# Values centred per head before a delta-rule recurrence, in place of means taken out of its outputs

## The chip, the core and the metric

The kernel runs on one core of a Trainium2 chip. The metric is device time in microseconds (us). The core has five engines that run side by side, each through its own list of instructions in order: TensorE (PE, matrix products), VectorE (DVE), ScalarE (ACT), GpSimd (POOL) and SyncE (SP, which issues most DMAs). An instruction waits on semaphores until what it needs is there, and everything behind it on the same engine waits too.

## What is computed

One layer of a hybrid backbone: 256 context and 1024 latent tokens, width 1024. A projection feeds two branches: (A) a bidirectional recurrence of the RWKV-7 kind with 16 heads of 64 channels, and (B) a bidirectional retention with 4 heads. Both are normed per head, projected, merged by gates and projected once more. What matters here, cut from the reference:

```python
def step(S, inp):                       # branch A, per head; S is (64 values) x (64 keys)
    w_t, k_t, v_t, kk_t, b_t = inp[:5]
    sa = jnp.einsum('bhvk,bhk->bhv', S, kk_t)
    S = (S * w_t[:, :, None, :] - sa[..., None] * b_t[:, :, None, :]
         + v_t[..., None] * k_t[:, :, None, :])
    o = jnp.einsum('bhvk,bhk->bhv', S, inp[5]) if with_out else None
...
o = head_norm((outs[0] + outs[1]).reshape(B, L, A_WIDTH), ln_w, ln_b, A_HEADS, A_GN_EPS)
o = o + (bons[0] + bons[1]).reshape(B, L, A_WIDTH).astype(o.dtype)
```

`head_norm` takes the mean over a head's 64 channels off, divides by the root of their variance, and scales and shifts per channel. The state `S` begins at zero, and each step is linear in `v` along the value axis: decay, the product with the keys and the read-out act on the key axis alone. So if each `v_t` has mean zero over its head's 64 channels, every row sum of `S` and every output `o` has mean zero too. The term `bons` uses `v` itself.

## The kernel before

Tokens lie along the free axis and channels on the 128 partitions, two heads (a "pair") to a tile, so that there are 8 pairs. Products in float32 are made of rounded parts: a tile is split into `hi` (a cast on ACT, line 210) and `lo` (the rest, a subtraction on DVE or POOL, line 211).

**Preparation** (lines 335 to 551, up to about 797 us): for each pair p, `stage_a` projects and convolves keys `kc` and values `vc`, norms the keys, and prepares the values for the recurrence (lines 440 to 457). For each of two directions the values (copied in reversed order for the second one) are transposed on PE in blocks of 128 tokens (line 451), copied from psum into a tile `vt` by ACT (line 452), and stored to the scratch tensor `vtD` by four DMAs on POOL's queue (line 456). `vt` has tokens on its partitions, and 10 blocks of 128 channels, 20 heads' worth of 64, along its free axis. Then come the scaled keys of each direction (`stage_a_dir`), with decays `cs` and products `bk`, `kr` on DVE. Between these, PE runs projections that nothing waits for soon: rope projections of retention's queries and keys (`rope_proj`), and gates. `vt` is one of 11 slots of a pool that most of the tiles of the preparation share.

**Recurrence** (`phase1b`, up to about 1775 us): chunks of 64 tokens, reads `vtD`, sums both directions into `oT` and stores `oD`. PE's order is pinned there.

**Second half** (`phase2`): `retention` goes over 4 heads, in each over chunks of 128 tokens. A chunk's scores are `sc` (line 1469), its output `ro` (lines 1477 and 1416 to 1418), its state update `st` with the result `s` (line 1431) on DVE. The output is normed (lines 1491 to 1496), transposed (`ot`, line 1502), scaled by ACT (`on`, line 1506), gated on POOL and stored to `orD` by SP. `out_a` projects branch A's output. In each of two halves of 512 tokens it first norms 8 tiles, `rwkv_norm` (lines 1296 to 1321): it loads `x`, takes sums over heads with `head_sums`, two products with a block matrix of ones, first of `x` for the mean (`mu`), then of the squares for the variance (`va`). Then it scales, adds the term `bon`, multiplies by the gate, and splits into an `act` tile. All 8 are needed for the projection `ya` (lines 1276 to 1278, 8 outputs of 24 products each per half). Only when retention's buffers are free does `phase3` load its operands: `act` tiles of `orD` (line 1266 ff.) through two buffers `ar`, `fn`, the gate row, `ma`, `mb` and `x`, all on SP's queue. They feed the products `yr`, then the last projection `po`.

What sets the order: the program is written as above, and the framework's scheduler interleaves it into one list per engine before the run, by its own model of durations. In the second half, retention, the norms and `ya` are therefore mixed on each engine.

The shared helper and the norm's own lines:

```python
def head_sums(self, acc, x, hl, eng=None):
    hi, lo = hl
    self.split(hi, lo, x, eng)
    self.nc.tensor.matmul(acc, self.ones, hi, start=True, stop=False)
    self.nc.tensor.matmul(acc, self.ones, lo, start=False, stop=True)
```

Of the kernel before, what the change touches and what calls it, by code (L numbers as in the profile page):

```python
# [8 lines left out]
F32 = mybir.dt.float32  # L9
F32R = mybir.dt.float32r  # L10
AF = mybir.ActivationFunctionType
ALU = mybir.AluOpType
# [3 lines left out]
P = 128  # L16
# [4 lines left out]
T = CTX + LAT  # L21
NPAIR = 8
C = 64
NU = T // C
# [19 lines left out]
MUE = 1  # L44
# [84 lines left out]
class Kern:  # L129
# [282 lines left out]
    def stage_a(self, p, wp, gps, bonus):  # L412
        nc, pv = self.nc, self.pv
        col = lambda base: pv[:, base + p:base + p + 1]
        ur = self.sa.tile([P, 2, 2, P], F32, tag="st", name=self.nm("ur"), bufs=3)
        nc.sync.dma_start(ur, self.ins["lup"][p])
        uh = self.l1.tile([P, 2, 2, P], F32R, tag="uph", name=self.nm("uph"), bufs=1)
        ul = self.upl
        nc.scalar.copy(uh, ur)
        nc.vector.tensor_tensor(ul[0:64], ur[0:64], uh[0:64].bitcast(F32), op=ALU.subtract)  # L420
        self.up = uh, ul
        kc = self.conv_proj(8 + p, 8 + p, False, wp, gps, "kc")
        self.filler_tile()
        vc = self.conv_proj(16 + p, 16 + p, False, wp, gps, "vc")
        self.filler_tile()
        bonus()

        sq = self.slot("sq")
        nc.scalar.activation(sq[:, :T], kc[:, :T], AF.Square, scale=col(PV_KK))
        hi, lo, rn = self.slot("sh", F32R), self.slot("sl", F32R), self.slot("rn")  # L430
        for (t0, n) in BLOCKS:
            a = self.aps.tile([P, 512], F32, tag="a", name=self.nm("ssk"))
            b = slice(t0, t0 + n)
            self.head_sums(a[:, :n], sq[:, b], (hi[:, b], lo[:, b]), SSE and nc.gpsimd)
            nc.scalar.activation(rn[:, t0:t0 + n], a[:, :n], AF.Ln, bias=self.eps[:, 3:4])
        nc.scalar.activation(rn[:, :T], rn[:, :T], AF.Exp, scale=-0.5)
        kk = self.slot("kk")
        nc.vector.scalar_tensor_tensor(kk[:, :T], kc[:, :T], col(PV_KK), rn[:, :T], op0=ALU.mult, op1=ALU.mult)

        for d in range(2):  # L440
            src = vc
            if d == 1:
                src = self.slot("vr")
                for a, b in ((0, CTX), (CTX, T)):
                    nc.scalar.copy(src[:, a:b], vc[:, a:b][:, ::-1])
            vt = self.slot("vt")
            for q in range(0, 10, 4):
                m = min(4, 10 - q)
                tp = self.tps.tile([P, 512], F32, tag="t", name=self.nm("vtp"))
                for i in range(m):  # L450
                    nc.tensor.transpose(tp[:, i * P:(i + 1) * P], src[:, (q + i) * P:(q + i + 1) * P], self.ident)
                nc.scalar.copy(vt[:, q * P:(q + m) * P], tp[:, :m * P])
            v4 = vt[:, :T].rearrange("q (t h c) -> q t h c", h=2, c=C)
            for h in range(2):
                for par in range(2):
                    nc.gpsimd.dma_start(self.vtD[p, d, h].rearrange("q (t a) c -> q t a c", a=2)[:, :, par, :],
                                        v4[64 * par:64 * par + 64, :, h, :])
        rc = self.conv_proj(p, p, True, wp, gps, "rc")
        self.filler_tile()
        kds = None  # L460
        for d in range(2):
            kds = self.stage_a_dir(p, d, kc, kk, rc, kds)
            self.filler_tile()
        self.gate_proj(24 + p, self.gD[p], True, wp, gps, self.sa)
        self.filler_tile()

        nc.vector.scalar_tensor_tensor(kds[:, CTX:T], kds[:, CTX:T], col(PV_RK), rc[:, :LAT], op0=ALU.mult, op1=ALU.mult)

        def bonus():
            bon, hi, lo = self.slot("bon"), self.slot("bh", F32R), self.slot("bl", F32R)  # L470
            for b in range(2):
                a = self.aps.tile([P, 512], F32, tag="a", name=self.nm("bon"))
                c = slice(512 * b, 512 * b + 512)
                self.head_sums(a, kds[:, CTX:][:, c], (hi[:, c], lo[:, c]), BNE and nc.gpsimd)
                nc.vector.scalar_tensor_tensor(bon[:, 512 * b:512 * b + 512], a, 0.5, vc[:, CTX + 512 * b:CTX + 512 * b + 512],
                                               op0=ALU.mult, op1=ALU.mult)
            nc.gpsimd.dma_start(self.bonD[p], bon[:, :LAT])
        return bonus
# [817 lines left out]
    def rwkv_norm(self, p, t0, ps):  # L1296

        nc = self.nc
        col = lambda base: self.ph[:, base + p:base + p + 1]
        psum = lambda name: ps.tile([P, 512], F32, tag="ps", name=self.nm(name), bufs=2)  # L1300
        x = self.ap.tile([P, 512], F32, tag="ar", name=self.nm("ar"), bufs=AR)
        self.load(x, self.oD[p][:, t0:t0 + 512])
        parts = lambda: [self.wp.tile([P, 512], F32R, tag=t, name=self.nm(t), bufs=b) for t, b in (("hi", WH), ("lo", WH))]
        pm = psum("mu")
        self.head_sums(pm, x, parts(), MUE and nc.gpsimd)
        nc.vector.scalar_tensor_tensor(x, pm, -1.0 / 64, x, op0=ALU.mult, op1=ALU.add)
        sq = self.wp.tile([P, 512], F32, tag="sq", name=self.nm("sq"), bufs=1)
        nc.scalar.activation(sq, x, AF.Square)
        pq = psum("va")
        self.head_sums(pq, sq, parts(), VAE and nc.gpsimd)  # L1310
        nc.scalar.activation(sq, pq, AF.Ln, bias=self.eps[:, 1:2], scale=1.0 / 64)
        nc.scalar.activation(sq, sq, AF.Exp, scale=-0.5)
        nc.vector.tensor_tensor(x, x, sq, op=ALU.mult)
        nc.vector.tensor_scalar(x, x, col(PV_LW), col(PV_LB), op0=ALU.mult, op1=ALU.add)
        for src, op in ((self.bonD, ALU.add), (self.gD, ALU.mult)):
            t = self.wp.tile([P, 512], F32, tag="ma", name=self.nm("bg"), bufs=2)
            self.load(t, src[p][:, t0:t0 + 512])
            nc.gpsimd.tensor_tensor(x, x, t, op=op)
        hl = self.ap.tile([P, 2, 512], F32R, tag=f"a{p}", name=self.nm("act"), bufs=1)
        self.split(hl[:, 0], hl[:, 1], x)  # L1320
        return hl
# [276 lines left out]
```

## Time and profile before

| | us |
|---|---|
| median of three runs | 2483.74 (2483.72 to 2492.42) |
| the profiled execution: its time | 2488.66 |
| its span, first to last instruction | 2486.9 |
| mean granted TensorE clock | 0.988 |
| PE busy, 100 to 300 us | 199.2 of 200 |
| DVE busy, 100 to 300, 300 to 500, 500 to 700 | 144.3, 154.1, 152.2 of 200 each |
| DVE busy, 1800 to 1900 | 84.5 of 100 |

The profile is of one execution. Its page gives busy time per engine; other views group instructions by line, operation and tile, list who waited for whom, show instructions in order of time, or give busy time by stretches. Names are the program's tile names: `mu<-hi,ones` is a product that writes `mu` from `hi` and `ones`. PEld is PE's loading of weights, which overlaps its products. A line can be that of a helper, so tiles tell more than lines. Queue issues appear as SPq or POOLq.

### The profile page before, as it was taken

The numbers are of one execution on the slowest core, as the hardware profiler recorded it, in microseconds if no ns is written. First come the engines' busy times: TensorE is split into PE (matmuls) and PEld (weight loads), VectorE is DVE, ScalarE is ACT, GpSimd is POOL, SyncE is SP. The second block draws the span as 40 slices with busy tenths as digits, with TensorE's granted clock in tenths as the row PEclk, the third lists the DMA queues.
The fourth block names the chain that finished last, engine by engine and source line by source line (L and its number), as shares of the span: only waits on it lengthen the run. The fifth ranks groups of instructions, "written<-read, shape, count | busy, mean of one in ns | idle before, by whom it ended". The sixth has DMA issues, their size and how long they took to land. (4 is left out here: it accounts for less than half of the span.)

```text
span 2486.9 us, 53478 instructions
## 1 busy us (share of the span) xinstructions
PE 2387.7 (96%) x21200; PEld 1926.9 (77%) x21200; DVE 1596.5 (64%) x2834; ACT 1159.9 (47%) x2547; POOL 575.0 (23%) x720
## 2 busy tenths in 40 slices
PE   7999999999999999998999999999898998999998
PEld 4888888888888899887777777777665765678786
DVE  5486787777666334353988777883378558745644
ACT  6434344434443444445665566644355435533422
POOL 2221111112122011111232222222276345400000
PEclk9999999999999999998999999999999999999999
DMA  6154454445446525344655566553465654575552
GB/s 251 50 161 116 138 163 132 131 151 142 127 143 191 175 73 147 99 135 131 171 161 173 151 180 180 157 159 116 132 200 175 204 170 152 169 272 178 182 174 85
DMA packets 337709, 385.07 MB, mean 155 GB/s; under 512 B 87467, under 2 KB 240819, under 8 KB 334387
## 3 DMA queue, kind: packets, MB, share of 16 engines
q1 hardware_dynamic: 304370, 298.80, 39.3%
q0 software_dynamic: 12992, 55.58, 8.5%
q10 hardware_dynamic: 20096, 27.27, 3.1%
q8 instruction: 167, 2.74, 0.5%
q14 instruction: 84, 0.68, 0.1%
HBM read 264.63 MB, written 116.92 MB: 153 GB/s over the span
## 5 line engine op out<-in xcount | busy, mean ns | idle before, releaser
L330 PE MATMUL gm<-uh,wh 128*128 128x512 f32 x896 | 351.2, 393 | 5.6 <-ACT xp L402 3.6
L331 PE MATMUL gm<-ul,wh 128*128 128x512 f32 x896 | 351.6, 392 | 0.7 <-DVE ul L299 0.7
L332 PE MATMUL gm<-uh,wl 128*128 128x512 f32 x896 | 351.2, 392 | 0.0
L1065 POOL TENSOR_TENSOR sp<-sv,pc 64x256 f32<-64x256 f32 x152 | 104.8, 690 | 428.4 <-DVE sv L1089 192.2
L330 PEld LDWEIGHTS gm<-uh,wh 128*128 128x128 f32 x896 | 168.1, 188 | 40.0 <-ACT xp L402 4.0
L331 PEld LDWEIGHTS gm<-ul,wh 128*128 128x128 f32 x896 | 168.4, 188 | 37.9 <-DVE xnt L298 1.7
L332 PEld LDWEIGHTS gm<-uh,wl 128*128 128x128 f32 x896 | 168.3, 188 | 34.3
L557 PE MATMUL gm<-uh,wlo 128*128 128x512 f32 x416 | 171.1, 411 | 0.7 <-DVE wlo L660 0.7
L557 PE MATMUL gm<-uh,whi 128*128 128x512 f32 x416 | 171.1, 411 | 0.0
L557 PE MATMUL gm<-ul,whi 128*128 128x512 f32 x416 | 170.7, 410 | 0.0
L660 DVE TENSOR_TENSOR wlo<-wraw,whi 128x256 fp32r<-128x256 f32 x168 | 79.2, 483 | 126.0 <-ACT whi L659 125.5
L557 PE MATMUL gv<-wlo,uh 128*128 128x256 f32 x512 | 148.4, 290 | 0.6 <-issue 0.6
L557 PE MATMUL gv<-whi,ul 128*128 128x256 f32 x512 | 148.5, 290 | 0.3 <-issue 0.3
L557 PE MATMUL gv<-whi,uh 128*128 128x256 f32 x512 | 148.1, 289 | 0.0
L211 DVE TENSOR_TENSOR lo<-raw,hi 128x512 fp32r<-128x512 f32 x128 | 92.6, 732 | 84.1 <-ACT hi L210 83.8
L210 ACT CAST hi<-raw 128x512 fp32r<-128x512 f32 x128 | 78.0, 620 | 130.1 <-PE yr L1277 62.3
L904 DVE TENSOR_TENSOR TL<-TL,tmp 128x31 f32<-128x31 f32 (+15 forms) x310 | 129.8, 419 | 8.1
L902 DVE TENSOR_TENSOR tmp<-E,TL 128x31 f32<-128x31 f32 (+15 forms) x310 | 129.2, 417 | 8.8
L1079 ACT COPY uv<-U 64x256 f32<-64x256 f32 x160 | 58.7, 367 | 149.6 <-PE U L557 87.0
L1477 PE MATMUL ro<-s,rs 128*128 128x512 f32 x256 | 123.4, 597 | 1.8 <-DVE s L1431 1.8
L1089 DVE TENSOR_TENSOR sv<-S,sp 64x256 f32<-64x256 f32 x144 | 60.7, 422 | 94.8 <-PE S L557 71.4
L210 ACT CAST wh<-wr 128x1024 fp32r<-128x1024 f32 x56 | 58.8, 1050 | 130.6 <-PE gm L331 103.3
(297 smaller groups left out, 6208.0 us busy)
## 6 DMA issues: line engine op xcount, KB each, us to landing
wr<-in_w_in SPq DMA_DIRECT2D x56, 512.0 KB
wraw<-in_w_in SPq DMA_DIRECT2D x84, 256.0 KB
bk<-bkD SPq DMA_DIRECT2D x80, 256.0 KB
krD<-kr POOLq DMA_DIRECT2D x16, 1024.0 KB, 4.6
raw<-in_wr SPq DMA_DIRECT2D x64, 256.0 KB
vtD<-vt POOLq DMA_DIRECT2D x64, 160.0 KB, 4.2
bkD<-bk POOLq DMA_DIRECT2D x32, 320.0 KB, 6.6
bkD<-bk POOLq DMA_DIRECT2D x16, 640.0 KB, 6.4
```

The costliest lines, as they stand in the source:

```text
L210: nc.scalar.copy(hi, src)
L211: (eng or nc.vector).tensor_tensor(lo, src, hi.bitcast(F32), op=ALU.subtract)
L330: nc.tensor.matmul(acc[:, :n], hi[:, k, :], self.hi(k, t0, n), start=(k == 0), stop=False)
L331: nc.tensor.matmul(acc[:, :n], hi[:, k, :], self.lo(k, t0, n), start=False, stop=False)
L332: nc.tensor.matmul(acc[:, :n], lo[:, k, :], self.hi(k, t0, n), start=False, stop=(k == KT - 1))
L557: return self.pin(self.nc.tensor.matmul(*a, **k))
L660: self.late(nc.vector.tensor_tensor(lo[:, j % size, k:k + 2], r, h.bitcast(F32), op=ALU.subtract), "v")
L902: self.late(nc.vector.tensor_tensor(t3, et[:, j + 1:, j:j + 1].broadcast_to([P, n, m]), tl[:, j:j + 1, 0:m].broadcast_to([P, n, m]), op=AL ...
L904: self.late(nc.vector.tensor_tensor(tl[:, j + 1:, 0:m], tl[:, j + 1:, 0:m], t3, op=ALU.subtract), "v")
L1065: nc.gpsimd.tensor_tensor(sp[ch], sv[ch, h], pcs[ch].broadcast_to([64, 4, C]), op=ALU.mult)
L1089: self.lead("v", nc.vector.tensor_tensor(new[h], ps[ch], sp[ch], op=ALU.add))
L1477: nc.tensor.matmul(po, qx[d][:, k, cols], st[:, k, :], start=(d == 1 and k == 0), stop=False)
```

## The change

In the preparation, after a direction's `vt` is complete, DVE now sums each head's 64 channels of every token (`vm`, 128x20) and subtracts a 64th of the sum in place. The four DMAs to `vtD` now follow that subtraction. In the group norm the mean's two products, their split (a cast on ACT, a subtraction on POOL), their psum tile and the subtraction of the mean on DVE are gone; the squares are taken of `x` as it is loaded. The term with `bon` reads `vc`, which is unchanged. Lines after the first piece are 6 higher in the changed kernel, after the second one 3 higher.

```diff
@@ -450,6 +450,12 @@
                     nc.tensor.transpose(tp[:, i * P:(i + 1) * P], src[:, (q + i) * P:(q + i + 1) * P], self.ident)
                 nc.scalar.copy(vt[:, q * P:(q + m) * P], tp[:, :m * P])
+
+            vm = self.sa.tile([P, NU], F32, tag="vm", name=self.nm("vm"), bufs=2)
+            v3 = vt[:, :T].rearrange("q (u c) -> q u c", c=C)
+            nc.vector.tensor_reduce(vm, v3, axis=mybir.AxisListType.X, op=ALU.add)
+            nc.vector.scalar_tensor_tensor(v3, vm.rearrange("q (u o) -> q u o", o=1).broadcast_to([P, NU, C]), -1.0 / C, v3,
+                                           op0=ALU.mult, op1=ALU.add)
             v4 = vt[:, :T].rearrange("q (t h c) -> q t h c", h=2, c=C)
             for h in range(2):
                 for par in range(2):
@@ -1301,9 +1307,6 @@
         self.load(x, self.oD[p][:, t0:t0 + 512])
         parts = lambda: [self.wp.tile([P, 512], F32R, tag=t, name=self.nm(t), bufs=b) for t, b in (("hi", WH), ("lo", WH))]
-        pm = psum("mu")
-        self.head_sums(pm, x, parts(), MUE and nc.gpsimd)
-        nc.vector.scalar_tensor_tensor(x, pm, -1.0 / 64, x, op0=ALU.mult, op1=ALU.add)
         sq = self.wp.tile([P, 512], F32, tag="sq", name=self.nm("sq"), bufs=1)
         nc.scalar.activation(sq, x, AF.Square)
         pq = psum("va")
```

The scheduler orders each engine's list anew. In the recurrence PE's list stays as it was; in the preparation it moves slightly, and in the second half retention, the norms and `ya` are interleaved in another way. The pieces that matter are shown in the prediction.

## The prediction

> **What bounds the kernel now.** I read the page's first line, then busy time by stretches, then what TensorE (PE) waits for.
>
> ```profile
> PE 2387.7 (96%) x21200; PEld 1926.9 (77%) x21200; DVE 1596.5 (64%) x2834; ACT 1159.9 (47%) x2547; POOL 575.0 (23%) x720
> ```
>
> PE is busy 96% of the span. The timeline shows how long a product really holds it:
>
> ```profile
> 1850.71 0.40 PE L217 MATMUL mu<-hi,ones 128*128 128x512 f32 x1
> 1850.94 1.02 PE L1477 MATMUL ro<-s,rs 128*128 128x512 f32 x2
> ```
>
> The first column is the start, the second the duration. The product lasts 0.40 us, but the next starts 0.23 us later: products overlap, so each costs 0.23 us of the engine's time.
>
> The change adds work in the preparation and takes work out of the second half. The next rows are stretches with us of busy time: length, PE, PEld, DVE (VectorE), ACT (ScalarE), POOL (GpSimd), then the granted clock, DMA share and GB/s.
>
> ```profile
> 300.00:500.00 200.00, 200.00 (x986) 168.14 (x986) 154.09 (x174) 87.65 (x132) 38.92 (x79) 1.00 0.49 139
> 1775.00:1800.00 25.00, 13.20 (x55) 9.98 (x54) 7.92 (x13) 10.68 (x18) 7.24 (x8) 0.80 0.62 184
> 1800.00:1820.00 20.00, 17.26 (x72) 11.35 (x71) 15.97 (x25) 9.44 (x19) 16.51 (x14) 1.00 0.63 198
> 1860.00:1880.00 20.00, 17.11 (x72) 11.45 (x71) 17.24 (x25) 14.31 (x32) 12.88 (x10) 1.00 0.78 231
> 1880.00:1900.00 20.00, 16.30 (x66) 11.19 (x65) 18.59 (x30) 11.11 (x22) 10.78 (x9) 0.92 0.27 86
> 2060.00:2080.00 20.00, 18.26 (x77) 11.98 (x76) 14.85 (x27) 12.70 (x29) 14.23 (x11) 1.00 0.68 213
> 2080.00:2100.00 20.00, 16.79 (x67) 11.98 (x66) 16.96 (x27) 9.54 (x19) 5.74 (x5) 0.91 0.30 95
> 2100.00:2120.00 20.00, 17.95 (x75) 11.58 (x74) 16.84 (x26) 11.77 (x27) 14.65 (x12) 1.00 0.38 115
> ```
>
> In the preparation (first row) PE does not pause at all and DVE has 46 us in 200 free. From 1800 to 2120 PE does pause: in the six rows from 1800 on it is idle 2.7 + 2.9 + 3.7 + 1.7 + 3.2 + 2.1 = 16.3 us. There only retention feeds PE while DVE is up to 93% busy, partly with the group norms.
>
> **What the change removes.** Of each of 16 group norms (8 pairs, 2 halves) go two products, ACT's cast, POOL's subtraction and DVE's removal of the mean.
>
> ```profile
> L210 ACT CAST hi<-ar x16: 607/618/638, 1805.5 to 2126.5; 128x512 fp32r<-128x512 f32 x16
> L1306 DVE SCALAR_TENSOR_TENSOR ar<-mu,ar x16: 665/680/692, 1810.5 to 2133.4; 128x512 f32<-128x512 f32 x16
> ```
> ```profile
> L211 POOL TENSOR_TENSOR lo<-ar,hi 128x512 fp32r<-128x512 f32 x16 | 21.5, 1346 | 28.9 <-ACT hi L210 27.8 <-DMA rs<-kD 1.1
> ```
>
> *PE's work:* 32 x 0.23 = **-7.4 us**, all on the path. *The pauses beside the norms:* 9.9 us of ACT, 10.9 of DVE and 21.5 of POOL go, and each norm's chain is shorter by 0.62 + 1.35 + 0.23 + 0.68 = 2.9 us and its hand-overs. Bounds: none of the 16.3 us, or all. I take **-6 us**, a little over a third, since the rest is retention's own chain. The clock falls to 0.92 and 0.91 in two of these rows: (0.08 + 0.09) x 20 = 3.4 us of cycles, of which I take **-1.5 us**.
>
> **What it adds.** For each of 16 pairs and directions DVE sums 128x1280 into 128x20 and subtracts the mean, between ACT's copies and POOL's stores of `vt`.
>
> ```profile
> L523 DVE SCALAR_TENSOR_TENSOR av<-av,kk 128x1280 f32<-128x1280 f32 x16 | 23.9, 1494 | 0.0
> L521 DVE TENSOR_SCALAR kd<-av,ph 128x1280 f32<-128x1280 f32 x16 | 14.2, 890 | 0.0
> L513 DVE TENSOR_TENSOR_SCAN cs<-scanm,cs 128x650 f32<-128x650 f32 x32 | 46.6, 1498 | 1.4
> ```
>
> The subtraction has L523's form: 1.49 us. A sum of this size is not in the trace: L521 (0.89 us) is its lower end, twice L513's 650 elements (3.0 us) the upper; I take 1.5, nearest to the other pass over 1280 elements. So 16 x 3.0 = 48 us of DVE (38 to 72). The Trainium skill ("VectorE: DVE Perf Modes", section on the perf-mode tier table) says a `tensor_reduce` has only the 1x mode, which at 0.96 GHz is an estimated 1.33 us; with it the 48 would be some 45.
>
> It lies beside PE's work if DVE's gaps hold it. One pair lasts 86 us, from one `kk` to the next (297.27 to 383.76); in brackets is how long DVE had waited:
>
> ```profile
> 297.27 1.55 DVE L438 SCALAR_TENSOR_TENSOR kk<-kc,pv,rn 128x1280 f32<-128x1280 f32 x1 [1.36 <-ACT rn L436]
> 333.79 0.83 DVE L511 TENSOR_SCALAR cs<-cs 128x1280 f32<-128x1280 f32 x1 [1.70 <-ACT cs L507]
> 339.76 1.23 DVE L542 TENSOR_TENSOR kr<-pe,kk 128x1024 f32<-128x1024 f32 x1 [2.12 <-issue]
> 383.76 1.55 DVE L438 SCALAR_TENSOR_TENSOR kk<-kc,pv,rn 128x1280 f32<-128x1280 f32 x1 [6.39 <-ACT rn L436]
> ```
>
> On DVE, pair 2's second direction stood so before (`bk` the scaled keys, `cs` the next direction's decays):
>
> ```order
> L523 SCALAR_TENSOR_TENSOR av_2478<-av_2478,kk_2364 128x1280
> L540 TENSOR_TENSOR kx_2522<-pe_2506,kk_2364 128x256
> L532 TENSOR_TENSOR bk_2515<-kd_2511,pi_2508 128x20x64
> L532 TENSOR_TENSOR bk_2515<-av_2478,pi_2508 128x20x64
> L511 TENSOR_SCALAR cs_2626<-cs_2626 128x20x64
> ```
>
> and now (lines are 6 higher there):
>
> ```order
> L529 SCALAR_TENSOR_TENSOR av_2496<-av_2496,kk_2376 128x1280
> L546 TENSOR_TENSOR kx_2540<-pe_2524,kk_2376 128x256
> L456 TENSOR_REDUCE vm_2422<-vt_2405 128x20
> L538 TENSOR_TENSOR bk_2533<-kd_2529,pi_2526 128x20x64
> L211 TENSOR_TENSOR wl_2867<-wr_2864,wh_2866 128x1024
> L538 TENSOR_TENSOR bk_2533<-av_2496,pi_2526 128x20x64
> L708 SCALAR_TENSOR_TENSOR gp_2759<-gp_2759,gm_2734 128x512
> L457 SCALAR_TENSOR_TENSOR vt_2405<-vm_2422,vt_2405 128x1280
> L517 TENSOR_SCALAR cs_2644<-cs_2644 128x20x64
> ```
>
> The two new rows fall where DVE waited 1.7 and 2.1 us; the first direction's fall into wide gaps between rope tiles. `bk` and `cs` queue behind them, and POOL's four `vtD` stores leave later with `vt`'s slot. Three waits for such a slot exist already:
>
> ```profile
> ACT av L510 <- DMA vtD<-vt: 8.9, 3, 4.1
> ```
>
> (us in all, times, longest). PE has other projections in hand (four psum tiles of 24 products each), so I take **+1.5 us**; bounds 0 and 8 x 2 = 16, a 3.0 us shift of each pair less a third found in gaps.
>
> **What it moves.** PE's order is unchanged through the recurrence. In the second half the norms end sooner, so `ya` starts sooner and is used up sooner. Before, around retention's last product (`ro`; `ot` its transposes, `yr` the next stage):
>
> ```order
> L1416 MATMUL ro_24262<-vt_23692,sx_24259 128x512
> L1417 MATMUL ro_24262<-vt_23692,sx_24259 128x512
> L1418 MATMUL ro_24262<-vt_23692,sx_24259 128x512
> L1502 MATMUL ot_24293<-ident,on_24222 128x128 x4
> L1278 MATMUL ya_25280<-act_25204,lo_25301 128x512
> L1276 MATMUL ya_25280<-act_25236,hi_25300 128x512
> ```
>
> and now:
>
> ```order
> L1419 MATMUL ro_24310<-vt_23740,sx_24307 128x512
> L1420 MATMUL ro_24310<-vt_23740,sx_24307 128x512
> L1421 MATMUL ro_24310<-vt_23740,sx_24307 128x512
> L1505 MATMUL ot_24341<-ident,on_24270 128x128 x4
> L1505 MATMUL ot_24354<-ident,on_24318 128x128 x4
> L1282 MATMUL yr_25579<-act_25501,hi_25581 128x512
> L1282 MATMUL yr_25661<-act_25501,hi_25663 128x512
> ```
>
> Before, 148 `ya` products stood between the last `ro` and the first `yr`; now none, and the last 55 rows ahead of `yr` hold none. What they covered:
>
> ```profile
> 2169.76 0.39 PE L1418 MATMUL ro<-vt,sx 128*128 128x512 f32 x1
> 2178.83 0.60 PE L1502 MATMUL ot<-ident,on 128*128 128x128 f32 x4
> 2205.40 0.40 PE L1276 MATMUL yr<-act,hi 128*128 128x512 f32 x1
> ```
> ```profile
> 2170.18 0.70 DVE L1491 BATCH_NORM_STATS2 bst<-ro 128x6 f32<-128x512 f32 x1 [1.27 <-PE ro L1418]
> 2170.92 0.18 DVE L1493 BATCH_NORM_AGGREGATE bmv<-bst 128x2 f32<-128x6 f32 x1
> 2173.98 0.80 DVE L1496 TENSOR_SCALAR on<-ro,bmv 128x512 f32<-128x512 f32 x1
> ```
> ```profile
> 2172.01 0.30 ACT L1494 ACTIVATE bmv<-bmv,eps 128x1 f32<-128x1 f32 x1
> 2172.70 0.22 ACT L1495 ACTIVATE bmv<-bmv 128x1 f32<-128x1 f32 x1
> 2179.47 1.51 ACT L1506 ACTIVATE on<-ot,ph 128x128 f32<-128x128 f32 x4 [1.92 <-PE ot L1502]
> 2183.49 1.14 ACT L210 CAST act<-ar 128x512 fp32r<-128x512 f32 x2
> 2195.49 0.62 ACT L210 CAST act<-ar 128x512 fp32r<-128x512 f32 x1 [3.51 <-DMA ar<-orD]
> 2206.87 1.16 ACT L210 CAST act<-ar 128x512 fp32r<-128x512 f32 x2 [1.41 <-DMA ar<-orD]
> ```
> ```profile
> 2184.91 0.61 SPq L1518 DMA_DIRECT2D fn<-in_fnw  x1
> 2195.49 1.91 SPq L1540 DMA_DIRECT2D x<-in_x  x3
> ```
> ```profile
> 2190.00:2200.00 10.00, 10.00 (x44) 8.08 (x43) 3.37 (x6) 2.76 (x5) 0.00 (x0) 1.00 1.03 361
> ```
>
> Between 2170 and 2205 PE ran `ya` while retention's last tile was normed, its buffers came free, and `yr`'s operands (`act`) were loaded and split. Four terms follow.
> - *Retention alone at its end,* four chunks of 6.2 us:
>
> ```profile
> 1839.70 0.60 PE L1469 MATMUL sc<-rs,rs 128*128 128x128 f32 x4
> 1845.86 0.60 PE L1469 MATMUL sc<-rs,rs 128*128 128x128 f32 x4
> ```
>
> (a chunk begins with `sc`): 25 us, at the 2.7 idle in 20 of 1800 to 1820, **+3.5 us** (2 to 5).
> - *The drain:* statistics 0.70 and 0.18, Ln 0.30, Exp 0.22, norm 0.80, transposes 0.60, copy 1.51, cast 0.62 = 4.9 us and hand-overs: **+6 us** (5 to 8).
> - *Operands late:* `act` tiles 1 and 2 are there at once, but their two buffers, and `x` and `fn` in SP's queue (now all ahead of tile 5), set the rest: before, 1 was cast at 2183.5, 3 at 2195.5, 5 at 2206.9. At the 361 GB/s of the last row the 2 MB to tile 4 (`fn` and the gate row 0.5 each, `ma`, `mb` and two tiles 0.25 each) take 6 us, the 3 MB from there to tile 6 (four `x` of 0.5, `ma`, `mb`, two tiles) another 8. Two interleaved `yr` use a pair in 12 x 0.23 = 2.8 us. So PE waits about 5, 5, then 2 for later pairs: **+12 us** (4 to 18).
> - *The clock* after such waits: 1775 to 1800 shows 0.80; at the 1.7 us per gap of the two rows at 0.92 and 0.91, **+2 us** (0 to 4). The Trainium skill ("TensorE: Matmul & The Clock Gate", Part 1) says that an idle window of about 3.4 us halves the clock until a busy one has passed; the drops agree with it, and by it two gaps would cost an estimated 3.4 us.
>
> **The sum:** -7.4 - 6 - 1.5 + 1.5 + 3.5 + 6 + 12 + 2 = +10.1 us. The profiled execution took 2488.66 us (span 2486.9), 4.9 over the median of the three runs, 2483.74, so it becomes 2498.8, and the median about **2493** (+0.4%). About 0.5%, 12.4 us, is what a measurement of this kernel can tell from no change.
>
> **The rivals.**
> - *The hand-over bites in full* (slower): retention's drain and `yr`'s loads at their upper ends, 8 + 18 + 4, a tail of 5, the pauses only 2 smaller: -7.4 - 2 + 1.5 + 5 + 30 = +27, **2511**. For it: DMA is full from 2190 on. Against: with `ya` gone, SP has fewer weights to fetch. It decides once PE waits over 20 us between the last `ro` and `act` 8.
> - *The work removed is what counts* (faster): operands 4, drain 5, tail 2, and 10 of the pauses go: -7.4 - 10 - 3 + 1 + 2 + 5 + 4 = -8, **2475**, or 2469 if all pauses go. For it: PE is 96% busy. Against: the order above.
> - *DVE sets the preparation* (slower): each pair ends 2 us late, 16 us in place of 1.5: **2508**. Against: 46 us free in 200. It decides when PE waits in the preparation exceed 10 us.
>
> **How the numbers follow.** Forecast 0.50 (2484 to 2502: 0.32 within 0.5%, 0.18 slower); full hand-over 0.18 (slower); removed work 0.24 (0.11 faster, 0.13 within); DVE 0.08 (0.05 slower, 0.03 within). Faster 0.11, within 0.48, slower 0.41. The range, 2472 to 2511, leaves out the best end of the third case and the worst of the others.
>
> **What would show it.** Right: PE waits of 5 us or more around the first `yr`, named `act` or `ar<-orD`; fewer pauses beside the norms; PE unbroken up to the recurrence. Wrong: a `yr` that follows the last `ro` within 3 us and runs on, or waits on DVE in the preparation. An `ot` or `act` wait of under 10 us in all would make the sum wrong.

## The result, and the profile after

The changed kernel takes **2516.72 us** (median of 4, 2514.39 to 2523.51) where the kernel before takes 2486.73 (median of 4, 2483.72 to 2492.42). The ratio is **1.0122 [1.0105, 1.0139]**: slower by 30 us, above the predicted range. The profiled execution took 2517.99 us, its span is 2516.2.

Three marks divide the span: the first product of the recurrence (`B`), the first `yr` and the last `yr`. These are the groups of products on `B` and on `yr`, the kernel before first; columns are durations in ns (min/median/max), then first and last start in us.

```profile
L557 PE MATMUL B<-kt,bi x1280: 218/218/366, 828.0 to 1602.6; 64*64 64x64 f32 x183
L1276 PE MATMUL yr<-act,hi x256: 388/394/500, 2205.4 to 2431.4; 128*128 128x512 f32 x128
L1278 PE MATMUL yr<-act,lo x256: 388/394/502, 2205.9 to 2431.9; 128*128 128x512 f32 x128
```

After:

```profile
L563 PE MATMUL B<-kt,bi x1280: 218/218/365, 844.5 to 1621.5; 64*64 64x64 f32 x183
L1282 PE MATMUL yr<-act,hi x256: 388/394/796, 2222.9 to 2460.7; 128*128 128x512 f32 x128
L1284 PE MATMUL yr<-act,lo x256: 387/394/628, 2224.9 to 2461.2; 128*128 128x512 f32 x128
```

The preparation is 16.5 us longer, the middle from `B` to `yr` (1377.4 before, 1378.4 after) 1.0, and the stretch from the first to the last `yr` (226.5 and 238.3) 11.8. Their sum, 29.3 us, is the whole growth of the span. So two places pay, and the work taken away in the middle brought no gain that shows.

Who PE waits for says where. These are rows of the whole span after (us in all, times, longest); rows of other stages, which stand in both kernels, are left out:

```profile
PE yr L1282 <- ACT act L210: 10.4, 4, 5.1
PE gm L330 <- ACT xp L402: 8.8, 3, 6.3
PE za L489 <- ACT av L516: 3.9, 1, 3.9
PE ot L1505 <- DVE on L1499: 3.6, 2, 3.3
PE gm L330 <- ACT rp L759: 1.9, 1, 1.9
```

Before, from 100 to 815 us:

```profile
PE gm L330 <- ACT xp L402: 3.6, 2, 2.8
PE gv L557 <- ACT whi L659: 2.2, 1, 2.2
PE gm L330 <- ACT rp L753: 1.4, 1, 1.4
```

In the preparation the waits of `gm` and `za` grew from 5.0 to 14.6 us. Busy time by stretches, after (length, PE, PEld, DVE, ACT, POOL, clock, DMA share, GB/s):

```profile
300.00:500.00 200.00, 199.47 (x981) 167.42 (x980) 163.11 (x181) 84.04 (x126) 34.45 (x69) 1.00 0.49 137
500.00:700.00 200.00, 187.82 (x915) 158.01 (x914) 156.07 (x173) 80.64 (x119) 44.65 (x72) 0.96 0.45 129
1794.00:2223.00 429.00, 397.25 (x1668) 270.85 (x1666) 291.24 (x457) 199.19 (x458) 187.12 (x146) 0.97 0.58 180
2225.00:2235.00 10.00, 4.92 (x13) 3.59 (x12) 1.27 (x2) 1.24 (x2) 0.00 (x0) 0.67 1.02 327
2235.00:2245.00 10.00, 7.44 (x19) 5.23 (x19) 2.74 (x5) 2.51 (x5) 0.00 (x0) 0.67 0.85 317
```

and before, the stretch that answers to the third row, from retention's first transposition to the first `yr`:

```profile
1776.00:2205.00 429.00, 400.86 (x1696) 275.87 (x1695) 292.06 (x471) 208.88 (x474) 204.89 (x162) 0.98 0.60 186
```

PE loses 12 us and clock in 500 to 700, a stretch in which DVE is not busier than in 300 to 500. Retention takes 429 us in both kernels: 3.6 us of PE's busy time went, and 3.6 us of idle time came (28.1 to 31.7).

**The one long stall of the preparation.** This is the timeline near 600 us, in pair 5 (start, duration, and in brackets how long the engine had waited and for whom): POOL, then DVE, then ACT.

```profile
594.55 6.72 POOL L525 COPY pc<-pe 128x20 f32<-128x20 f32 x1 [11.24 <-ACT pe L521]
601.22 2.80 POOL L462 DMA_DIRECT2D vtD<-vt  x4
```
```profile
588.77 1.49 DVE L456 TENSOR_REDUCE vm<-vt 128x20 f32<-128x1280 f32 x1
590.17 2.91 DVE L519 TENSOR_TENSOR_SCAN cs<-scanm,cs 128x650 f32<-128x650 f32 x2
592.99 1.47 DVE L457 SCALAR_TENSOR_TENSOR vt<-vm,vt 128x1280 f32<-128x1280 f32 x1
594.38 0.88 DVE L527 TENSOR_SCALAR kd<-av,ph 128x1280 f32<-128x1280 f32 x1
...
599.71 1.48 DVE L538 TENSOR_TENSOR bk<-av,pi 128x1280 f32<-128x1280 f32 x1
```
```profile
607.45 1.05 ACT L516 ACTIVATE av<-za,ph 128x256 f32<-128x256 f32 x2 [10.71 <-DMA vtD<-vt]
```

The last copy into `vt` ends at 588.7. The subtraction is done at 594.5, since the scans of `cs` stand between it and the sum. POOL then has the small `pc` copy ahead of the stores: it takes 6.72 us and ends, at 601.27, when DVE's run of operations ends (599.71 + 1.48). Only then are the four `vtD` stores issued; ACT's `av` waits 10.71 us for the slot that they free, PE waits 3.9 us for `av` and then 6.3 for `xp`, and the clock falls to 0.5 from 610 to 620. In the kernel before, the same stores were issued ahead of the `pc` copy:

```profile
584.79 2.81 POOL L456 DMA_DIRECT2D vtD<-vt  x4 [12.53 <-ACT vt L452]
587.45 0.86 POOL L519 COPY pc<-pe 128x20 f32<-128x20 f32 x1
```

So the added pass did not only make the stores later by its own time; it put them behind another operation on POOL.

### The profile page after: what moved, and what is told of

The parts are those of the page before. It is cut to its first block, busy times and chain, and to the rows that moved or that the text cites. A ratio compares the mean times of both kernels' runs of the same rounds, so it can differ in the third digit from the quotient of the medians.

```text
span 2516.2 us, 53352 instructions
## 1 busy us (share of the span) xinstructions
PE 2397.9 (95%) x21168; PEld 1930.5 (77%) x21168; DVE 1639.0 (65%) x2850; ACT 1151.4 (46%) x2531; POOL 558.5 (22%) x704
## 4 chain that ended last, share of the span: by engine, by line
PE 54%; DMA 6%; issue 6%; DVE 4%; POOL 2%; ACT 2%; SPq 1%; POOLq 0%; ACTq 0%; DVEq 0%
PE gm L563 10%; PE gv L563 8%; PE A L563 3%; PE gm L330 3%; PE gm L331 2%; PE gm L332 2%; PE yr L1282 2%; PE yr L1283 2%; PE yr L1284 2%; PE S L563 2%; PE X L563 2%; PE ro L1480 2%; PE bt L1051 2%; DMA ar<-orD 2%; DMA bi<-bkD 1%
```

## Experiments

Each is timed beside the kernel before on the same chip (its medians: 2486.6 to 2489.3 us). The marks are of one profiled execution each, which can lie far from its kernel's median (a_first's is the fastest of ten runs, norm_only's the slowest of six); the change of each of the three stretches against the kernel before is in us. Some kernels have the same order of instructions on every engine in the preparation: norm_only that of the kernel before, and x_late, a_first and centre_only that of the changed kernel. Two such executions, with the `pc` copy held in both or in neither, differ by 0.5 to 2.2 us there. The recurrence, whose PE order is the same in all, took from 947 to 961 us, so the column on the middle is not read as an effect of the edits.

| | ratio | median | preparation | middle | first to last `yr` |
|---|---|---|---|---|---|
| the change | 1.0122 [1.0105, 1.0139] | 2516.7 | +16.5 | +1.0 | +11.8 |
| centre_only | 1.0037 [1.0015, 1.0058] | 2496.4 | +8.5 | -0.2 | -0.8 |
| norm_only | 1.0059 [1.0041, 1.0078] | 2504.1 | +2.1 | +2.9 | +15.6 |
| x_late | 1.0104 [1.0089, 1.0119] | 2514.2 | +14.3 | -0.4 | +12.4 |
| two_reduces | 1.0092 [1.0072, 1.0112] | 2513.6 | +6.1 | +4.6 | +15.0 |
| pc_act | 1.0078 [1.0052, 1.0104] | 2511.3 | +5.9 | -1.8 | +12.8 |
| centre_pe | 1.0152 [1.0127, 1.0178] | 2528.3 | +15.5 | +3.8 | +14.9 |
| a_first | 1.0051 [1.0031, 1.0070] | 2504.0 | +8.0 | -3.5 | -0.7 |
| both | 1.0098 [1.0077, 1.0119] | 2516.5 | +17.9 | +10.1 | +0.1 |
| four_reduces | 1.0165 [1.0139, 1.0191] | 2528.9 | +27.3 | +0.3 | +14.2 |
| best1 | 1.0081 [1.0053, 1.0109] | 2507.5 | +17.3 | +2.9 | -1.4 |
| best3 | 1.0070 [1.0043, 1.0098] | 2507.8 | +8.7 | +5.1 | -1.7 |
| a_first_pc | 1.0031 [1.0019, 1.0044] | 2495.6 | +7.3 | +5.7 | -2.0 |
| before_pc | 0.9992 [0.9981, 1.0002] | 2485.5 | -0.5 | -4.8 | +1.9 |

**Theory 1:** the preparation pays, as the stores of the values go out later. **Theory 2:** the first `yr` products wait for operands that could not be loaded earlier. **Rivals:** VectorE's load by itself; the scheduler's other order; the hand-over alone; full DMA queues.

**The centring alone** (centre_only).

```diff
+        pm = psum("mu")
+        self.head_sums(pm, x, parts(), MUE and nc.gpsimd)
+        nc.vector.scalar_tensor_tensor(x, pm, -1.0 / 64, x, op0=ALU.mult, op1=ALU.add)
         sq = self.wp.tile([P, 512], F32, tag="sq", name=self.nm("sq"), bufs=1)
```

> The values are centred as in the changed kernel, and the group norm keeps its products for the means, so the output is the reference's. Theory 1 (the preparation pays: the stores of the centred values go out later, a buffer comes free later, TensorE stalls near 605 us): the last `bon` product stays near 819 us (798 before), the second half is that of before, 2504 to 2509 us. Rival (the hand-over to the last projection pays for all of it, and the preparation's loss is made good later): within 5 us of 2487.

The preparation pays, but 8.5 us, not 16.5; the median is 8 us under what was expected. Yet in the preparation every engine's order is that of the changed kernel. The same place on POOL and DVE:

```profile
593.10 0.78 POOL L525 COPY pc<-pe 128x20 f32<-128x20 f32 x1 [11.24 <-ACT pe L521]
593.83 2.80 POOL L462 DMA_DIRECT2D vtD<-vt  x4
```
```profile
592.93 0.88 DVE L527 TENSOR_SCALAR kd<-av,ph 128x1280 f32<-128x1280 f32 x1
```

In both executions the copy starts 0.17 us after `kd`'s first pass does. Here it takes 0.78 us, ends as `kd`'s first pass ends (593.81), and the stores go out at once; there it was held through the rest of DVE's run. The stores go out 6 us sooner (601.22 - 593.83, less 1.45 by which the whole place lies earlier), and the two preparations differ by 8, or by 6.5 without the 1.45 that came before. Two more executions of the same order say the same: in x_late and a_first this copy starts at 593.21 and 593.22 and takes 6.72 and 0.78 us, and the first `B` comes at 842.3 and 836.0. So the held copy costs 6.3 to 6.5 us. Without it PE still waits at this place, now only for `xp`:

```profile
PE gm L330 <- ACT xp L402: 8.6, 3, 5.9
```

The wait for `av` is gone, and the clock granted from 605 to 620, in steps of 5 us, is 0.88, 0.50 and 0.94 instead of 0.69, 0.50 and 0.50. Of this kernel's seven runs six lie between 2493 and 2500 us and one at 2512. The Trainium skill ("SBUF — State Buffer", section "SBUF: two separate sides") says that a DVE operation with two inputs in SBUF and a GpSimd operation that reads SBUF exclude each other, whichever comes first holding the ports for the whole instruction. The trace agrees that the copy is kept out, with 6.72 us against 0.78; here that went on through the run of several DVE instructions, not one. That these ports are the reason is not shown by a run; that DVE's run and the copy end together is.

**The norm alone** (norm_only).

```diff
-            vm = self.sa.tile([P, NU], F32, tag="vm", name=self.nm("vm"), bufs=2)
...
-            nc.vector.tensor_reduce(vm, v3, axis=mybir.AxisListType.X, op=ALU.add)
...
```

> No centring of the values; the group norm has no products for the means, so the mean stays in its outputs and the output is not the reference's. Theory 1: the preparation ends near 798 us as before, and what is left is the removed products against the uncovered first `yr` products: 2496 to 2500 us, with TensorE waiting about 10 us for `act` near 2205 us. Rival (the removed work is worth its 15 us, and the hand-over costs nothing once the preparation is right): 2470 to 2480 us.

15 us slower, with the preparation nearly that of before (+2.1): taking the products away is a loss by itself, a little larger than expected. `yr` waits 11.0 us for `act`. The rival that removed work counts has fallen, and so has the one that the hand-over makes up the whole loss, as the centring alone costs 8. Its order in the preparation is that of the kernel before, so the +2.1 there is the difference between two executions.

**The loads of `x` later** (x_late).

```diff
-                nc.sync.dma_start(x, ins["x"][CTX + t0 + P * t:CTX + t0 + P * t + P, :])
+                self.late(nc.sync.dma_start(x, ins["x"][CTX + t0 + P * t:CTX + t0 + P * t + P, :]), "w")
...
-        self.load(raw, src)
+        self.lead("w", self.load(raw, src))
```

> The changed kernel with the four loads of `x` (2 MB, needed only by the output projection) queued behind the weights' loads instead of among the first loads of `ar`. If the wait of the first `yr` products is for `ar` held up by `x` in the transfers (theory 2): the 10 us of waits for `act` fall to 2 to 5 us, 2506 to 2511 us. Rival (the bandwidth is full there anyway, and weights take the place of `x`): within 3 us of 2517.

The time is the rival's: 2.5 us under the changed kernel, and the stretch of `yr` is as long as there (238.9 us). The waits for `act` fell only to 8.4. `x` was not what stood in the way: ACT waits 9.54 us for the second pair of `ar`, and 9.67 in the changed kernel. The rival's reason, a full bandwidth, is not shown either, as the DMA share here is 0.87 and 0.47 in the two stretches of 10 us from 2221. (Its `pc` copy was held for 6.72 us too.)

**VectorE's load without the held stores** (two_reduces).

```diff
-            nc.vector.scalar_tensor_tensor(v3, vm.rearrange("q (u o) -> q u o", o=1).broadcast_to([P, NU, C]), -1.0 / C, v3,
-                                           op0=ALU.mult, op1=ALU.add)
+            nc.vector.tensor_reduce(vm, v3, axis=mybir.AxisListType.X, op=ALU.add)
```

> As the changed kernel, but the subtraction is replaced by a second, equal reduction: VectorE does as much, the stores of the values don't wait for it; the mean stays in, so the output is not the reference's. If VectorE's load alone slows the preparation (rival 1): last `bon` product near 817 us and 2513 to 2519 us. If it is the held stores (theory 1): last `bon` near 800 us, 2496 to 2502 us.

Between the two: the median is what the load's rival gave, the preparation (+6.1) lies nearer to theory 1's. Against the norm alone the two sums cost 4.0 us of preparation (8 us by the two ratios); with the stores waiting (the centring alone) the same DVE time costs 6.4. The difference is hardly more than that between two executions of one order, so a cost of waiting behind the subtraction as such does not show. What is not the held copy looks like DVE's load, but the edit brought another order on every engine with it. The next run raises the dose.

**Twice that load** (four_reduces).

```diff
-            nc.vector.tensor_reduce(vm, v3, axis=mybir.AxisListType.X, op=ALU.add)
-            nc.vector.tensor_reduce(vm, v3, axis=mybir.AxisListType.X, op=ALU.add)
+            for _ in range(4):
+                nc.vector.tensor_reduce(vm, v3, axis=mybir.AxisListType.X, op=ALU.add)
```

> Four equal reductions of the values on VectorE in place of one reduction and one subtraction (96 us of VectorE instead of 48), nothing subtracted, so the mean stays in and the output is not the reference's. With two of them the first `B` product came at 834.1 us against 830.1 without any. If VectorE's load sets the loss, it grows with the dose, and faster, as the stalls add up: first `B` at 840 to 850 us, 2515 to 2530 us. If the order that came with the edit made the loss: about 834 us and 2513 us again.

`B`, and PE's waits up to 815 us:

```profile
L562 PE MATMUL B<-kt,bi x1280: 218/218/363, 855.3 to 1632.3; 64*64 64x64 f32 x183
```
```profile
PE gm L330 <- ACT xp L402: 19.6, 6, 6.5
```

830.1, 834.1, 855.3 us for none, two and four sums: the first 48 us of DVE cost 4, the next 48 cost 21, more than was expected. By the ratios to the kernel before (1.0059, 1.0092, 1.0165) it is some 8 and 18 us. PE's waits for `xp` grow with the dose, 4.2, 5.9 and 19.6 us, and no `pc` copy was held with four sums (the longest took 1.27 us). That speaks for the load; but each of the three has its own order of instructions on every engine, so the order is not ruled out as a part of it. DVE was busy 597.9 of the 720 us from 100 to 820 here, 561.5 with two sums, 520.8 before.

**The copy off POOL** (pc_act).

```diff
-        nc.gpsimd.tensor_copy(self.pc[:, p, d, :], pe3[:, :, C])
+        nc.scalar.copy(self.pc[:, p, d, :], pe3[:, :, C])
```

> The changed kernel with GpSimd's small `pc` copy given to ScalarE, so that the stores of the values don't stand behind it. In the changed kernel that copy took 6.72 us in pair 5 (it ended when VectorE's run of operations ended), and 0.78 us at the same place of the same order in the kernel that only centres. If that copy is what made the preparation lose 8 us more there: first `B` product near 836 us instead of 844.5, 2507 to 2510 us. If the subtraction alone holds the stores: first `B` near 844 us, 2515 to 2518 us.

The order is nearly that of the changed kernel. Near what was expected in the preparation (`B` at 833.9), and 1 us above the range in the median. With the stores still behind the subtraction, the preparation costs 5.9 us, as much as with the two sums, where no store waited for DVE (+6.1).

**The centring on TensorE** (centre_pe).

```diff
+            nc.vector.scalar_tensor_tensor(self.cent, ones, -1.0 / C, self.ident, op0=ALU.mult, op1=ALU.add)
...
-                    nc.tensor.transpose(tp[:, i * P:(i + 1) * P], src[:, (q + i) * P:(q + i + 1) * P], self.ident)
+                    nc.tensor.matmul(tp[:, i * P:(i + 1) * P], src[:, (q + i) * P:(q + i + 1) * P], self.cent, start=True, stop=True)
...
-            nc.vector.tensor_reduce(vm, v3, axis=mybir.AxisListType.X, op=ALU.add)
```

> The changed kernel with the centring moved to TensorE: the transposition of the values is a product with the identity less 1/64 in each head's block, and VectorE's reduction and subtraction are gone; the output is the reference's. An fp32 product of 128 columns (`sc`) and a transposition (`ktp`) both follow the one before by 0.11 us, so TensorE should pay nothing. If VectorE's 48 us and the held stores are the preparation's whole loss: first `B` product at 828 to 831 us and 2501 to 2506 us, as without the centring. If an order of instructions that came with the edit costs it: first `B` above 836 us.

The expectation failed: `B` came at 843.5, and the median is 2528.3. These are the groups of `vtp` in the changed kernel, then here:

```profile
L451 PE MATMUL vtp<-ident,vc x80: 270/272/274, 103.9 to 759.7; 128*128 128x128 f32 x80
```
```profile
L453 PE MATMUL vtp<-cent,vc x160: 270/275/275, 103.9 to 755.3; 128*128 128x128 f32 x160
```

A transposition is one row of the trace, an fp32 product of the same size two; `sc`, from which the price was taken, has two rows for each product as well. So 160 rows came to PE, 160 x 0.11 = 17.6 us of its path, and the preparation is 15.5 us longer although PE's waits for `xp` are down to 2.6 us. As PE is the bound there, this says nothing for or against DVE's load: most of the waits went, and the products cost more.

**Heads 0 and 1 first** (a_first).

```diff
-            orr = [self.act(self.orD, k, t0, f"or{k}", ac) for k in range(8, 16)]
-            orr += [self.act(self.orD, k, t0, f"a{k}") for k in range(8)]
+            orr = [self.act(self.orD, k, t0, f"a{k}") for k in range(8)]
+            orr += [self.act(self.orD, k, t0, f"or{k}", ac) for k in range(8, 16)]
...
-                    self.prod(pr, self.weights(ins["wr"][m][:, (g + 8) % 16:(g + 8) % 16 + 4]), orr[g:g + 4], g == 0, g == 12)
+                    self.prod(pr, self.weights(ins["wr"][m][:, g:g + 4]), orr[g:g + 4], g == 0, g == 12)
```

> The changed kernel with the last projection's terms in another order: heads 0 and 1 of the retention (written long before) first, heads 2 and 3 last, so that eight of the sixteen operands can be loaded while the retention still runs. Theory 2 (the first `yr` products wait for operands that could not be loaded before the retention's end): waits for `act` near 2225 us fall from 10 us to under 3 us and first to last `yr` from 238 to about 228 us, 2504 to 2508 us. Rival (the transfers of weights, or the low clock after the pause at the retention's last `ot`, set it): 2513 to 2518 us.

Theory 2 holds. The loads of `ar`, and of `x` among them, in SP's queue in the changed kernel, then here up to the same point:

```profile
2108.13 0.33 SPq L580 DMA_DIRECT2D ar<-orD  x1
2116.78 0.32 SPq L580 DMA_DIRECT2D ar<-orD  x1
2226.21 1.47 SPq L580 DMA_DIRECT2D ar<-orD  x2
2229.09 3.62 SPq L1543 DMA_DIRECT2D x<-in_x  x4
2234.45 0.97 SPq L580 DMA_DIRECT2D ar<-orD  x2
```
```profile
2095.78 0.33 SPq L580 DMA_DIRECT2D ar<-orD  x1
2104.25 0.32 SPq L580 DMA_DIRECT2D ar<-orD  x1
2172.49 0.92 SPq L580 DMA_DIRECT2D ar<-orD  x2
2177.46 1.67 SPq L580 DMA_DIRECT2D ar<-orD  x2
2181.86 1.69 SPq L580 DMA_DIRECT2D ar<-orD  x2
2186.48 2.19 SPq L580 DMA_DIRECT2D ar<-orD  x2
2215.64 1.72 SPq L580 DMA_DIRECT2D ar<-orD  x2
```

and PE's waits from 2160 to 2270 here:

```profile
PE ot L1505 <- DVE on L1499: 3.3, 1, 3.3
PE ot L1505 <- ACT on L1509: 1.1, 1, 1.1
PE yr L1282 <- ACT hi L210: 0.6, 1, 0.6
```

Ten `ar` loads are issued by 2189 us, ahead of the first `yr` (2209.9). In the changed kernel it was two, and the third came 3 us behind the first `yr`. Those two show what stood in the way: they were issued at 2108 and 2117, but ACT cast them only at 2222.26, just as its last work on retention's output ended. The tiles of heads 2 and 3 lie in a pool that opens where retention's ends, and until then the two `ar` buffers stay full; those of heads 0 and 1 lie in the pool of `ya`'s operands. The edit thus changed both which data come first and which buffers take them, and no run separates the two. No wait for `act` is left and the stretch of `yr` is 225.8 us, as before the change. The ten runs lie between 2492 and 2511 us.

**Both edits** (both; the two diffs above).

> The two edits together, centring on TensorE and heads 0 and 1 first. If both theories hold and the two losses add: 2489 to 2496 us, and the kernel before, 2486 to 2489 us, is matched and not clearly beaten, as the removed work was given back in the retention. If only the preparation's holds: 2501 to 2506 us.

It has the preparation of the centring on TensorE (+17.9) and the `yr` stretch of heads 0 and 1 first (+0.1). Its gain over the centring on TensorE, 11.8 us, is near the one that the second edit brought alone, 12.7. The median, 2516.5, is above both expected ranges, as the price of the product was wrong.

**VectorE's work given to ScalarE.** To heads 0 and 1 first and the moved copy, best1 adds

```diff
-        nc.vector.tensor_scalar(kd[:, :T], av[:, :T], -1.0, colk, op0=ALU.add, op1=ALU.mult)
+        nc.scalar.mul(kd[:, :T], av[:, :T], colk)
...
-        nc.vector.scalar_tensor_tensor(kd[:, :T], kd[:, :T], 1.0, kc[:, :T], op0=ALU.add, op1=ALU.mult)
+        nc.vector.scalar_tensor_tensor(kd[:, :T], kd[:, :T], self.onek[:, p:p + 1], kc[:, :T], op0=ALU.add, op1=ALU.mult)
```

(`onek` is 1 minus the factor `colk`, computed once, so that the result is the same.)

> The changed kernel with heads 0 and 1 first in the last projection, the `pc` copy on ScalarE, and one pass of each `kd` moved from VectorE to ScalarE (16 of 0.88 us, 14 us of VectorE). If the preparation's loss is VectorE's load: first `B` near 832 us, 2490 to 2498 us, between the kernel before and the one with heads 0 and 1 first alone (2504). If ScalarE's added work delays as much: 2500 to 2506 us.

and best3 the step on `cs` as well:

```diff
-        nc.vector.tensor_scalar(cs3[:, :, 1:C + 1], cs3[:, :, 1:C + 1], 1.0, 0.5, op0=ALU.add, op1=ALU.mult)
+        nc.scalar.activation(cs3[:, :, 1:C + 1], cs3[:, :, 1:C + 1], AF.Copy, scale=0.5, bias=0.5)
```

> As the one with `kd` moved, and the affine step on `cs` too (16 of 0.82 us more off VectorE, on ScalarE instead): VectorE's added load is then half made good. If the loss is VectorE's load: first `B` at 829 to 832 us and 2486 to 2496 us, about the kernel before. If ScalarE becomes the one waited for (its steps stand between `z` products and the scans): first `B` above 836 us, over 2500 us.

The times hoped for were missed by both; best3 came out as its rival said (`B` at 836.7, 2507.8 us). Both are slower than the same kernel without them, below: the preparation is 17.3 and 8.7 us longer, against 7.3 there, although DVE is busy 549.9 and 536.4 us from 100 to 820 instead of 560.1. PE's `gm` waits 11.6 and 8.6 us for ACT's psum copies `xp`, where it waits 6.7 without the added passes. Load taken off DVE was worth nothing here. That ACT's longer queue is why is argued: the order on every engine changed as well, and in best3 the preparation is only 1.4 us longer, which is within the difference of two executions.

**Heads 0 and 1 first, and only the copy moved** (a_first_pc; the diffs of a_first and pc_act).

> Heads 0 and 1 first in the last projection, and the `pc` copy on ScalarE, nothing else moved. With heads 0 and 1 first alone the runs lay between 2492 and 2511 us; if those near 2510 are the ones in which GpSimd's `pc` copy is held by VectorE's operations, taking it off GpSimd leaves 2492 to 2500 us and few runs above 2503. If that copy is not what spreads them: a median of 2500 to 2506 us again, spread as before.

The first expectation holds: all six runs lie between 2493.5 and 2500.0 us, median 2495.6. So the held copy also made much of the spread of 19 us; not all spread is its, since the four runs of pc_act, without heads 0 and 1 first, lay between 2506 and 2517. This is the best form of the change, and still slower than the kernel before by 0.3%.

**The copy moved in the kernel before** (before_pc; the diff of pc_act).

> The kernel before, without the change, with the `pc` copy on ScalarE. In its trace that copy was held once too, for 7.39 us at 688.6 us, just where TensorE paused 1.7 us. If the hold costs only where the stores behind it free a buffer that is waited for, as in the changed kernel's pair 5: no change here, 2484 to 2489 us. If it costs wherever it happens: 2479 to 2483 us, and the change's own loss, with that copy moved, is larger than the 9 us measured against the kernel before as it is.

No difference that can be told (0.9992, interval over 1), and the preparation is the same (-0.5). Held at 688.6 us, for 7.39 us, the copy cost nothing that can be measured; what follows it on POOL there is no store of `vt`. The total says less than the preparation, as the second half has another order here: from retention's first transposition to the first `yr` it took 417.6 us instead of 429.5, and the recurrence 6.9 more. An order of instructions alone can thus be worth as much as the operands' loss; no run was made to test that. No version was found that is measurably faster than the kernel before.

## Why the prediction was wrong

- *The preparation,* +1.5 us: **the step that failed.** It measured +16.5. Its prices were right: the sum took 1.48 us and the subtraction 1.48, where 1.5 and 1.49 were taken. Wrong was that the work lies in DVE's gaps, read from "46 us free in 200". That row, 300 to 500, had no pause of PE; but the kernel before already waited 2.8 us for `xp` at 604.9, in pair 5, and there the changed kernel lost most. The free share says nothing of who waits for an operation, and the sum counted the added work as if each gap were at its place. The runs show two parts in place of the 1.5. The held `pc` copy, behind which the subtraction had put the stores, costs 6.3 to 6.5 us (same order with and without the hold). Without the hold 8.0 and 8.5 are left (a_first, centre_only); two sums without the subtraction cost 6.1, so most of this is put down to DVE's load, with the new order not ruled out. The rest of the 16.5 is within the 2 us by which executions differ. The upper bound was right to half a microsecond, but by another mechanism than a shift in each pair: the loss sits in few pauses, chiefly those in pair 5 from 604 to 618 us.
- *The rival "DVE sets the preparation"* had its condition, PE waits over 10 us, met by 14.6 us. It got 0.08, and it was priced as an alternative to the hand-over's terms. The two happened together: with 16 in place of 1.5 the sum would have been +24.6. (The sum as written, 2483.74 + 10.1, gives 2493.8, where the forecast says 2493.)
- *The removed work,* -7.4, *the pauses,* -6, *their clock,* -1.5, *retention alone,* +3.5, *the drain,* +6: together -5.4; the stretch from retention's first transposition to the first `yr` came out at -1.0 (429.5 and 428.5 us; 429.7 in centre_only, which has the order of before there, and 428.5 to 429.8 in three more runs with the order of after). The drain was right: 6.9 us from the last `ro` (2216.0) to `yr`. Sized wrongly was the rest: idle time up to the last `ro` fell 1.8 us (28.1 to 26.3) where 6 were taken, and the clock granted up to there is 0.98 in both, where a gain of 1.5 us was taken. With the norms gone sooner, other stretches have retention alone: PE is busy 14.95 of 20 us from 2040 to 2060. That this is why is argued from the rows; no run separates it.
- *Operands late,* +12, and *the clock,* +2: measured +11.8 together, with the waits for `act` that were named. Right in size and place. The part that named `x` and `fn` as what delays the tiles was wrong for `x`, as `x` behind the weights changed nothing; `fn` was not moved. The cause is that all operands of the first products but two were loaded after the retention's end, and these two could not be cast before it.
- *The recurrence,* from the first `B` to retention's first transposition, took 2.0 us more (947.9 and 949.9); nothing was foreseen. Others differ by more (947.4 in a_first's execution, 954.7 in a_first_pc's), so it is not put down to the change; what makes it differ stays open.
- *"PE unbroken up to the recurrence"* was given as the sign that the sum is right. It was broken by 14.6 us of waits, where the kernel before had 5.0, and that alone would have told the error.

## What to carry to other kernels

Before work is booked as hidden on an engine that is partly idle, follow what waits for its result: here the added pass stood between a buffer's last write and its stores, the stores fell behind a copy that DVE's run could hold up, and one late group of them cost 6 us. Ask of work that is taken away what it covered, and where the cover is lost, let the next stage begin with the operands that are ready first and whose buffers are free; that one edit gave back the 12 us. Free time on an engine was not used up evenly: the first 48 us of load cost 4 to 8 us, the next 48 cost 18 to 21, each with an order of its own. And compare an edit with a second execution of the same order before a few us are put down to it.

## What the runs showed of the hardware

- A GpSimd copy of 128x20 took 0.78 us or 6.72 us at the same place of the same order, in two executions each, and started 0.17 to 0.18 us into the same DVE pass in all four; the short one ended with that pass, the long one with DVE's run. With the copy on ScalarE, where it takes 0.21 us, the runs of one kernel lay within 6.5 us instead of 19.
- An fp32 product of 128x128 by 128 columns is two rows of the trace at 0.11 us each, a transposition of that size one.
- PE's pauses cost more than themselves: from 605 to 620 us, with waits of 3.9 and 6.3 us, the clock granted was 0.69, 0.50 and 0.50, and with one wait of 5.9 us at that place 0.88, 0.50 and 0.94.
